# The product of p moved to the start of a decoder block, stores issued from another queue, four blocks stored as parts

## The chip, the cores and the metric

The kernel runs on one core of one Trainium2 chip. Its time is the device time of one execution in microseconds (us), and a version is judged by the median of several executions. The core has a matrix engine (TensorE, PE in the profile, with PEld for its weight loads), three engines for elementwise work (VectorE, DVE; ScalarE, ACT; GpSimd, POOL), and SyncE (SP), which here only issues DMA transfers. Each engine takes its instructions in the order of its own list and waits on semaphores; a DMA can be issued from the list of SP or, as the changed kernel does more, of POOL.

## The reference

All operands are float32. For T = 1024 tokens of width 1024 the block computes

```python
h = rms_norm(x, g_pre)
u, v, z_a, q, f, inp, z_b, a_a, a_b = split(h @ w_in)         # nine times 1024 columns
y_a = spatial_gating(gelu(u), layer_norm(gelu(v))) * silu(z_a)
y_b = rms_norm(hgrn2(silu(q), f, inp)) * silu(z_b)            # 8 heads, chunks of 32 tokens
merged = sigmoid(a_a) * (y_a @ w_branch_a) + sigmoid(a_b) * (y_b @ w_branch_b)
x = x + rms_norm(merged @ w_out, g_post)
e = p @ w_ple                                                  # (1024, 256) @ (256, 1024)
x = x + rms_norm(e * sigmoid(x @ w_ple_gate + b_ple_gate), g_ple)
```

The product e depends on the inputs p and w_ple alone and is used only in the last line.

## The kernel before

Every float32 operand of a product is split into a high part (`hi`, a cast to float32r, made by ACT at line 133) and a low part (`lo`, operand minus `hi`, made by DVE at line 134). A product is then three matmuls: high by low, low by high, high by high. The large products are made with seven block products in place of eight (`pair`): left and right sides are cut into 2 x 2 blocks, sums of blocks are formed, and the seven right-hand blocks are called b11, t4, t2, t1, t3, b21 and b22 in the order of use. Each block is a `slot`, a pair of 1 MB tiles (`...h` and `...l`), of which seven are on chip: x00, x01, x10, x11 and t0, t1, t2. One block product with a weight is 12 matmuls of 128 x 128 by 512 columns at line 748.

The stages, in order of time in the profile:

1. Start (0 to about 53 us). x is loaded in eight tiles `xt`, two per quarter, normalised by ACT and DVE, and transposed by PE (line 108) into the blocks of h. The first token product (lines 204 to 206, `token_first`) follows the transposes closely. `WARM` matmuls on zeros (line 104) stand ahead of all.
2. Token stage (to about 217 us): the columns `inp` and v of the projection, stored to DRAM as `v_sp` (line 351) and `vn_sp` (line 359) by way of token rooms `tq`. POOL forms sums of blocks of w_out and stores them (`wo_t`, line 497). DVE forms the sums of h's blocks (`sums`).
3. Projections (217 to 880 us): 28 pairs of columns in the order of the list "F0 Q0 U0 ZA0 ... ZB3 AB3", with the eight HGRN2 heads (`head`) woven in. Results go through eight buffers `q` (`quarter_tile`, QS = 8) to DRAM: f_sp, q_sp, u_sp, ga_sp, gb_sp by `stored` (line 839), bf_sp by `mix_b`, and in ZA the seven blocks of the first branch's input by `spill` (af_sp). A head reloads its F, Q and V.
4. The product e (880 to 908 us): w_ple is loaded and split into slot x00, p is loaded in pairs of token tiles into q buffers, transposed by PE, split, multiplied (lines 955 to 957), copied by ACT and stored as `e_sp`.
5. First branch (from 908 us): the seven blocks are read back by `fill`, which loads half a block into a raw buffer (three of these, RAWS = 3), and splits it into its slot; `weight_product` then runs four rounds (jp = 0 to 3) of seven block products.
6. Second branch, w_out product, gate (to 1270 us). The gate reloads e_sp.

The order of instructions on each engine comes from a scheduler that follows the order in which the program is written, with buffers and dependences as its limits. All transfers go through SP's list except the stores of `wo_t`. The splits of weights use five `hi` and five `lo` buffers (`unit`, UNITS = 5).

Of the kernel before, what the change touches and what calls it, by code (L numbers as in the profile page):

```python
# [8 lines left out]
F32 = mybir.dt.float32  # L9
# [16 lines left out]
AHEAD = 2  # L26
# [7 lines left out]
def hybrid_block(  # L34
# [45 lines left out]
    af_sp = {n: dram.tile([P, 4, 512], F32, name=f"af_{n}") for n in ("b11", "b21", "b22", "t1", "t2", "t3", "t4")}  # L80
# [153 lines left out]

    xts = [sp.tile([P, D], F32, name=f"xt{t}") for t in range(NT)]
# [103 lines left out]
    xb, xq = pool("xb", bufs=1, side="right")  # L339
# [6 lines left out]
    def to_heads(c0, g, r):  # L346

        h = c0 // P
        v = r.rearrange("p (t c) -> p t c", t=2)
        for i in range(2):  # L350
            nc.sync.dma_start(out=v_sp[h + i][:, 2 * g:2 * g + 2, :], in_=v[:, :, i * P:(i + 1) * P])

    def to_norm(c0, g, r):

        j = c0 // 256
        v = r.rearrange("p (t c) -> p t c", t=2)
        for t in range(2):
            nc.vector.bn_stats(out=stats[:, 2 * g + t, j, :], in_=v[:, t, :])
        nc.sync.dma_start(out=vn_sp[j][:, 2 * g:2 * g + 2, :], in_=v)
# [157 lines left out]
    nc.sync.dma_start(out=wT_sp, in_=wT)  # L517
# [18 lines left out]
    nc.sync.dma_start(out=badd_sp, in_=badd)  # L536
# [23 lines left out]
    def head(h):  # L560
# [170 lines left out]
        nc.sync.dma_start(out=b_sp[h], in_=z)  # L731
# [106 lines left out]
    def stored(dst, half, q):  # L838
        nc.sync.dma_start(out=dst[:, half * 512:(half + 1) * 512], in_=q)

    def projection(kind, jp):
# [21 lines left out]
        def mix_b(i, half, q):  # L863
            nc.scalar.activation(out=q, in_=q, func=AF.Silu)
            nc.vector.tensor_tensor(out=q, in0=q, in1=reload(b_sp[2 * jp + i], half), op=ALU.mult)
            nc.sync.dma_start(out=bf_sp[jp][:, i, half * 512:(half + 1) * 512], in_=q)
# [3 lines left out]
        def spill(n, t):  # L870
            nc.sync.dma_start(out=af_sp[n][:, jp, :], in_=t)
# [56 lines left out]
    wple = fill("x00", w_ple.rearrange("(k p) c -> p k c", p=P), [P, 2, D], "wple")  # L928
    first = pair_load(row_parity(w_branch_a), 0)
    pins, p_ready = {}, []  # L930

    def e_parts(t):
        if t % 2 == 0:
            pins[t // 2] = quarter_tile().rearrange("p (t c) -> p t c", t=2)
            nc.sync.dma_start(out=pins[t // 2], in_=p[t * P:(t + 2) * P, :].rearrange("(t p) c -> p t c", p=P))
        pt = small()
        for k in range(2):
            transpose(pt[:, k * P:(k + 1) * P], pins[t // 2][:, t % 2, k * P:(k + 1) * P])
        ph, pl = (a[:, 0:2, :] for a in unit(4))
        split(ph, pl, pt[:, 0:256].rearrange("p (k t) -> p k t", k=2))  # L940
        p_ready.append((ph, pl))

    for t in range(AHEAD):
        e_parts(t)
    for t in range(NT):
        if t + AHEAD < NT:
            e_parts(t + AHEAD)
        ph, pl = p_ready[t]
        pe = dense_tile()
        if t % 2 == 0:  # L950
            ev = xp.tile([P, 2, D], F32, tag=("x11h", "x11l")[t // 2 % 2], name="ev")
        for h in range(2):
            s = slice(h * 512, (h + 1) * 512)
            for k in range(2):
                nc.tensor.matmul(out=pe[h], lhsT=pl[:, k, :], rhs=wple[0][:, k, s], start=(k == 0), stop=False)
                nc.tensor.matmul(out=pe[h], lhsT=ph[:, k, :], rhs=wple[1][:, k, s], start=False, stop=False)
                nc.tensor.matmul(out=pe[h], lhsT=ph[:, k, :], rhs=wple[0][:, k, s], start=False, stop=(k == 1))
        for h in range(2):
            nc.scalar.copy(out=ev[:, t % 2, h * 512:(h + 1) * 512], in_=pe[h])
        if t % 2:  # L960
            nc.sync.dma_start(out=e_sp[t // 2], in_=ev)
# [25 lines left out]
    B = [fill(tag, bf_sp[k], [P, 2, T], f"B{k}") for k, tag in enumerate(("x01", "t1", "t0", "t2"))]  # L987
# [6 lines left out]
    for j in range(8):  # L994
# [6 lines left out]
        if j < 3:  # L1001
            n, tag = (("b11", "x10"), ("t4", "x11"), ("t2", "x00"))[j]
            o_blocks[n] = fill(tag, wo_sp[n] if j else wo[0][:, :, 0:512], [P, 4, 512], f"wo_{n}")
# [5 lines left out]
    def rest_of_blocks():  # L1009
        for n, tag, src in (("t1", "x01", wo_sp["t1"]), ("t3", "t1", wo_sp["t3"]),  # L1010
                            ("b21", "t0", wo[1][:, :, 0:512]), ("b22", "t2", wo[1][:, :, 512:1024])):
            o_blocks[n] = fill(tag, src, [P, 4, 512], f"wo_{n}")
# [23 lines left out]
    def x1T(t):  # L1036

        tag = ("t1h", "t1l", "t0h", "t0l")[t % 4]
# [9 lines left out]
    for tp in range(4):  # L1048
# [5 lines left out]
        if tp == 3:  # L1054
            wg = []
            for k, tag in enumerate(("x10", "x11", "x00", "x01")):
# [88 lines left out]
```

## Time and profile before

| | |
|---|---|
| median of 3 runs | 1273.06 us (1271.33 to 1277.49) |
| the profiled execution | 1271.88 us, its span 1270.2 us |
| PE busy | 1218.4 us, 96% of the span |
| PEld busy | 1018.5 us |
| DVE, ACT, POOL busy | 913.9, 601.4, 49.1 us |
| DMA moved | 184.07 MB, mean 145 GB/s |
| chain that ended last | PE 70%, DVE 12%, DMA 10%, ACT 5% |

The span is the time between the first and the last instruction of the profiled execution; 1.7 us of its time lie outside. A busy share is an average over all stages. The chain is the sequence of work that ended last, followed back from the end.

### The profile page before, as it was taken

Reading aid. Unit: us, or ns where it says so; the run is one execution under the profiler, and the core shown is the slowest. Engines: PE = TensorE matmul, PEld = TensorE weight load, DVE = VectorE, ACT = ScalarE, POOL = GpSimd, SP = SyncE. Lnnn points to the kernel's source line nnn. Section 1 sums busy time; section 2 is a strip of 40 time slices with the busy share of each in tenths; the row PEclk is TensorE's granted clock in tenths of the full one; section 3 lists DMA queues with packets and bytes.
Section 4 is the critical chain, followed back from the end, with each engine's and each line's share of the span. In section 5 each row is a group of like instructions: output and inputs, shape, how many; then the busy total and the mean of one; then the engine's idle time right before and its main releaser. Section 6 shows DMA issues by size and latency. Waiting matters only on the chain.

```text
span 1270.2 us, 20163 instructions
## 1 busy us (share of the span) xinstructions
PE 1218.4 (96%) x7640; PEld 1018.5 (80%) x7640; DVE 913.9 (72%) x1797; ACT 601.4 (47%) x1045; POOL 49.1 (4%) x94
## 2 busy tenths in 40 slices
PE   7899899999999999999999999999989999999997
PEld 6899898878778787887878788887768788887886
DVE  7986556678886888868686868655476753889866
ACT  5443333655665456645456545545643420545422
POOL 5025100000000000000000000000000000000000
PEclk8999989999999999999999999999989999999999
DMA  6347422435545354452443434346763771515231
GB/s 216 117 150 228 154 100 84 131 109 175 171 140 171 120 164 148 151 191 75 158 134 119 134 114 158 105 136 199 248 184 125 259 246 34 166 34 192 90 99 68
DMA packets 122966, 184.07 MB, mean 145 GB/s; under 512 B 8266, under 2 KB 76402, under 8 KB 122356
## 3 DMA queue, kind: packets, MB, share of 16 engines
q1 hardware_dynamic: 121588, 178.58, 42.8%
q0 software_dynamic: 1280, 4.20, 0.8%
q8 instruction: 60, 0.98, 0.3%
q14 instruction: 38, 0.31, 0.1%
HBM read 124.28 MB, written 58.46 MB: 144 GB/s over the span
## 4 chain that ended last, share of the span: by engine, by line
PE 70%; DVE 12%; DMA 10%; ACT 5%; issue 2%; SPq 0%; DVEq 0%; POOL 0%; ACTq 0%
PE big L748 39%; PE big L168 7%; PE small L108 2%; PE big L1078 2%; PE big L1080 2%; PE big L1079 2%; PE big L205 2%; PE big L206 2%; DVE lo L134 2%; PE big L204 2%; DMA Q<-q_sp 1%; DMA raw<-af_t 1%; PE small L205 1%; PE small L206 1%; PE small L204 1%
## 5 line engine op out<-in xcount | busy, mean ns | idle before, releaser
L134 DVE TENSOR_TENSOR lo<-S,hi 128x512 fp32r<-128x512 f32 x168 | 120.0, 718 | 83.4 <-ACT hi L133 82.2
L133 ACT CAST hi<-S 128x512 fp32r<-128x512 f32 x168 | 103.0, 618 | 153.4 <-PE big L748 100.8
L133 ACT CAST hi<-raw 128x512 fp32r<-128x512 f32 x122 | 75.1, 620 | 147.4 <-PE big L748 73.1
L134 DVE TENSOR_TENSOR lo<-raw,hi 128x512 fp32r<-128x512 f32 x122 | 83.2, 687 | 59.0 <-ACT hi L133 58.8
L771 DVE TENSOR_TENSOR q<-big,q 128x512 f32<-128x512 f32 x128 | 86.0, 685 | 12.7 <-PE big L748 11.7
L757 ACT COPY q<-big 128x512 f32<-128x512 f32 x108 | 62.8, 582 | 26.2 <-PE big L748 22.1
L752 DVE TENSOR_TENSOR S<-raw 128x512 f32<-128x512 f32 x64 | 44.0, 688 | 23.3 <-DMA raw<-in_w_in_dram 14.7
L748 PE MATMUL big<-t1l,hi 128*128 128x512 f32 x112 | 44.8, 400 | 1.9 <-ACT hi L133 1.9
L748 PE MATMUL big<-h00l,hi 128*128 128x512 f32 x112 | 45.1, 403 | 0.7 <-ACT q L757 0.7
L748 PE MATMUL big<-h11l,hi 128*128 128x512 f32 x112 | 45.3, 405 | 0.0
L748 PE MATMUL big<-t3l,hi 128*128 128x512 f32 x112 | 45.1, 403 | 0.0
L748 PE MATMUL big<-t2l,hi 128*128 128x512 f32 x112 | 45.1, 402 | 0.0
L748 PE MATMUL big<-h10l,hi 128*128 128x512 f32 x112 | 44.8, 400 | 0.0
L748 PE MATMUL big<-t0l,hi 128*128 128x512 f32 x112 | 44.8, 400 | 0.0
L748 PE MATMUL big<-t0h,hi 128*128 128x512 f32 x112 | 44.6, 398 | 0.0
L748 PE MATMUL big<-h00h,hi 128*128 128x512 f32 x112 | 44.6, 398 | 0.0
L748 PE MATMUL big<-t1h,lo 128*128 128x512 f32 x112 | 44.6, 398 | 0.0
L748 PE MATMUL big<-t0h,lo 128*128 128x512 f32 x112 | 44.5, 397 | 0.0
L748 PE MATMUL big<-t1h,hi 128*128 128x512 f32 x112 | 44.3, 396 | 0.0
L748 PE MATMUL big<-h10h,hi 128*128 128x512 f32 x112 | 44.3, 396 | 0.0
L748 PE MATMUL big<-h00h,lo 128*128 128x512 f32 x112 | 44.3, 396 | 0.0
L748 PE MATMUL big<-t2h,lo 128*128 128x512 f32 x112 | 44.1, 394 | 0.0
(559 smaller groups left out, 3691.4 us busy)
## 6 DMA issues: line engine op xcount, KB each, us to landing
raw<-in_w_in_dram SPq DMA_DIRECT2D x66, 512.0 KB, 3.9
xt<-in_x_dram SPq DMA_DIRECT2D x8, 512.0 KB, 8.9
v_sp<-tq SPq DMA_DIRECT2D x32, 128.0 KB, 3.6
wo_t<-t POOLq DMA_DIRECT2D x16, 256.0 KB, 4.0
vn_sp<-tq SPq DMA_DIRECT2D x16, 256.0 KB, 2.4
V<-v_sp SPq DMA_DIRECT2D x8, 512.0 KB, 4.5
f_sp<-q SPq DMA_DIRECT2D x16, 256.0 KB, 2.1
F<-f_sp SPq DMA_DIRECT2D x8, 512.0 KB, 3.6
```

The lines of the kernel that those rows point to most:

```text
L108: nc.tensor.transpose(out=o, in_=i, identity=ident[:n, :n])
L133: nc.scalar.copy(out=hi, in_=src)
L134: nc.vector.tensor_tensor(out=lo, in0=src, in1=hi.bitcast(F32), op=ALU.subtract)
L168: nc.tensor.matmul(out=ps[c0 // 512][:, c0 % 512:c0 % 512 + n], lhsT=wt(k), rhs=a(k, c0, n), start=(k == 0 and i == 0), stop=(k == NK - 1 ...
L204: nc.tensor.matmul(out=o, lhsT=al, rhs=hi, start=first, stop=False, **kw)
L205: nc.tensor.matmul(out=o, lhsT=ah, rhs=lo, start=False, stop=False, **kw)
L206: nc.tensor.matmul(out=o, lhsT=ah, rhs=hi, start=False, stop=last, **kw)
L748: nc.tensor.matmul(out=o, lhsT=w[:, k, :], rhs=x_[:, k, :], start=(k == 0 and i == 0 and not onto), stop=(k == 3 and i == 2), skip_group_c ...
L752: nc.vector.tensor_tensor(out=o, in0=x_, in1=y, op=op)
L757: nc.scalar.copy(out=o, in_=src)
L771: nc.vector.tensor_tensor(out=o, in0=x_, in1=y, op=ALU.add)
L1078: nc.tensor.matmul(out=o, lhsT=parts[:, 1, k, :], rhs=wh, start=(k == 0), stop=False)
```

## The change

The product e is made in the setup, quarter by quarter: `pins` (p) and the two halves of w_ple are loaded ahead of x, and a function `embedding(tp)` between the loads of a quarter of x and its normalisation makes one quarter of e and stores it. It uses buffers of the pool `xq` that the slots t1 and t2 take later. The first weights of the token stage are split with ACT's cast where DVE cast before, and the tile `sq` has one buffer where it had two. The stores v_sp, vn_sp, wT_sp, badd_sp, b_sp, bf_sp, af_sp and all of `stored` are issued by POOL (`nc.gpsimd`) where SP issued them. Four of the seven blocks of the first branch (`PARTED`) are split by `spill`, stored as two tensors, and read back by a plain DMA into their slot; the slots are handed out in another order, so that each block takes the slot that the block of the same turn had in the projections.

```diff
-AHEAD = 2
+PARTED = ("b11", "t2", "t3", "b22")
...
+    pins = xq.tile([P, NT, 256], F32, tag="t1h", name="pins")
+    wple = [sp.tile([P, 2, D], F32R, name=f"wple{n}") for n in "hl"]
+    for tp in range(4):
+        nc.sync.dma_start(out=pins[:, 2 * tp:2 * tp + 2, :],
+                          in_=p[tp * 256:(tp + 1) * 256, :].rearrange("(t p) c -> p t c", p=P))
+        if tp < 2:
+            raw = wp.tile([P, D], F32, tag="raw", name="raw", bufs=RAWS)
+            nc.sync.dma_start(out=raw, in_=w_ple[tp * P:(tp + 1) * P, :])
+            split(*(a[:, tp, :] for a in wple), raw)
+
+    def embedding(tp):
+
+        pt = small()
+        for t in range(2):
+            for k in range(2):
+                transpose(pt[:, (2 * t + k) * P:(2 * t + k + 1) * P], pins[:, 2 * tp + t, k * P:(k + 1) * P])
+        ph, pl = unit(4)
+        split(ph, pl, pt.rearrange("p (k t) -> p k t", k=4))
+        ev = xq.tile([P, 2, D], F32, tag=("t2h", "t2l")[tp % 2], name="ev")
+        for t in range(2):
+            for h in range(2):
+                pe = big()
+                s = slice(h * 512, (h + 1) * 512)
+                for k in range(2):
+                    for i, (w, a) in enumerate(((wple[0], pl), (wple[1], ph), (wple[0], ph))):
+                        nc.tensor.matmul(out=pe, lhsT=a[:, 2 * t + k, :], rhs=w[:, k, s], start=(k == 0 and i == 0),
+                                         stop=(k == 1 and i == 2))
+                nc.scalar.copy(out=ev[:, t, s], in_=pe)
+        nc.sync.dma_start(out=e_sp[tp], in_=ev)
...
+        embedding(quarter)
...
-            sq = sp.tile([P, D], F32, tag="sq", name="sq", bufs=2)
+            sq = sp.tile([P, D], F32, tag="sq", name="sq")
...
-            first.append(units_of(raw, split_dve))
+            first.append(units_of(raw, split))
...
     def stored(dst, half, q):
-        nc.sync.dma_start(out=dst[:, half * 512:(half + 1) * 512], in_=q)
+        nc.gpsimd.dma_start(out=dst[:, half * 512:(half + 1) * 512], in_=q)
...
         def spill(n, t):
-            nc.sync.dma_start(out=af_sp[n][:, jp, :], in_=t)
+            if n not in PARTED:
+                nc.gpsimd.dma_start(out=af_sp[n][:, jp, :], in_=t)
+                return
+            parts = unit(1)
+            split(*(a[:, 0, :] for a in parts), t)
+            for a, dst in zip(parts, af_parts[n]):
+                nc.gpsimd.dma_start(out=dst[:, jp, :], in_=a[:, 0, :].bitcast(F32))
...
-    for n, tag in (("b11", "x01"), ("t4", "t1"), ("t2", "t0"), ("t1", "t2"), ("t3", "x10"), ("b21", "x11"), ("b22", "x00")):
-        a_blocks[n] = fill(tag, af_sp[n], [P, 4, 512], f"a_{n}")
+    for n, tag in (("b11", "x00"), ("t4", "x01"), ("t2", "t1"), ("t1", "t0"), ("t3", "t2"), ("b21", "x10"), ("b22", "x11")):
+        if n in PARTED:
+            a_blocks[n] = slot(*at(tag), [P, 4, 512], f"a_{n}")
+            for part, src in zip(a_blocks[n], af_parts[n]):
+                nc.sync.dma_start(out=part.bitcast(F32), in_=src)
+        else:
+            a_blocks[n] = fill(tag, af_sp[n], [P, 4, 512], f"a_{n}")
```

The rest of the diff takes out the stage of the product e between the projections and the first branch, changes `nc.sync` to `nc.gpsimd` at the other stores named, and renames the slots that later blocks take.

SP's list at the start, before. Rows name what is written and what is read: `xt` are the tiles of x, `raw` buffers for weights.

```order
L96 DMA rows_g<-in_g_pre_dram 8x128
L244 DMA xt_202<-in_x_dram 128x1024
L244 DMA xt_203<-in_x_dram 128x1024
L190 DMA raw<-in_w_in_dram 128x4x256
L244 DMA xt_204<-in_x_dram 128x1024
L244 DMA xt_205<-in_x_dram 128x1024
L190 DMA raw<-in_w_in_dram 128x4x256
L244 DMA xt_206<-in_x_dram 128x1024
L244 DMA xt_207<-in_x_dram 128x1024
L244 DMA xt_208<-in_x_dram 128x1024
L244 DMA xt_209<-in_x_dram 128x1024
```

The same place in the changed kernel. `pins` is p, `ev` a finished quarter of e.

```order
L240 DMA pins<-in_p_dram 128x2x256
L244 DMA raw<-in_w_ple_dram 128x1024
L240 DMA pins<-in_p_dram 128x2x256
L244 DMA raw<-in_w_ple_dram 128x1024
L240 DMA pins<-in_p_dram 128x2x256 x2
L276 DMA xt_224<-in_x_dram 128x1024
L276 DMA xt_225<-in_x_dram 128x1024
...
L191 DMA raw<-in_w_in_dram 128x4x256
L276 DMA xt_228<-in_x_dram 128x1024
L265 DMA e_sp_142<-ev 128x2048
L276 DMA xt_229<-in_x_dram 128x1024
```

Six transfers, four of p and two of w_ple, now stand ahead of the first tile of x, and the store of the first quarter of e between x's tiles.

PE's list at the start, before: `rows_g` is g_pre, line 204 the first token product.

```order
L108 MATMUL small<-ident,rows_g 128x8
L108 MATMUL small<-ident,xt_202 128x128 x4
L108 MATMUL small<-ident,xt_203 128x128
...
L108 MATMUL small<-ident,xt_202 128x128
L108 MATMUL small<-ident,xt_203 128x128
L204 MATMUL big<-hi,h00l 128x256
L205 MATMUL big<-lo,h00h 128x256
L206 MATMUL big<-hi,h00h 128x256
```

The same place in the changed kernel; the lines left out repeat the three matmuls of line 262 or the transposes of the same two tiles.

```order
L109 MATMUL small<-ident,rows_g 128x8
L109 MATMUL small<-ident,pins 128x128 x4
L262 MATMUL big<-wpleh,lo 128x512
L262 MATMUL big<-wplel,hi 128x512
L262 MATMUL big<-wpleh,hi 128x512
...
L109 MATMUL small<-ident,xt_224 128x128 x4
L109 MATMUL small<-ident,xt_225 128x128
...
L109 MATMUL small<-ident,pins 128x128 x4
L262 MATMUL big<-wpleh,lo 128x512
...
L109 MATMUL small<-ident,xt_226 128x128
L109 MATMUL small<-ident,xt_227 128x128
```

Four transposes of p and 24 matmuls of e now stand ahead of x's first transposes, three more such lumps follow between x's quarters, and the token products (lines 205 to 207 now) come only after all of x's transposes.

SP's list between the projection AB3 and the first branch, before: `af_...` are the stored blocks of the branch's input, `gb_sp` the results of AB3.

```order
L810 DMA raw<-in_w_branch_a_dram 128x4x256 x2
L825 DMA raw<-af_b_125 128x1024 x2
L935 DMA q<-in_p_dram 128x2x256 x3
L839 DMA gb_sp_149<-q 128x512 x2
L839 DMA gb_sp_148<-q 128x512
L935 DMA q<-in_p_dram 128x2x256
L825 DMA raw<-af_t_131 128x1024
L839 DMA gb_sp_148<-q 128x512
L825 DMA raw<-af_t_131 128x1024
L961 DMA e_sp_138<-ev 128x2048
```

The same place in the changed kernel.

```order
L867 DMA q<-b_sp_75 128x512 x2
L972 DMA a_b11l<-af_b11l 128x2048
L842 DMA raw<-in_w_branch_a_dram 128x4x256
L972 DMA a_b11h<-af_b11h 128x2048
L857 DMA raw<-af_t_127 128x1024
L972 DMA a_t2h<-af_t2h 128x2048
L972 DMA a_t2l<-af_t2l 128x2048
L972 DMA a_t3h<-af_t3h 128x2048
L857 DMA raw<-af_t_127 128x1024
L857 DMA raw<-af_t_126 128x1024 x2
L972 DMA a_t3l<-af_t3l 128x2048
L857 DMA raw<-af_b_125 128x1024 x2
```

The loads of p and the stores of e and of AB3's results are gone from here, and blocks b11, t2, t3 and b22 come as two transfers each, straight into their slots (`a_b11l`, `a_b11h` and so on).

## Rows read from the trace of the kernel before

**Rows 1.** The page, part 1: busy us, share of the span, instructions.

```profile
PE 1218.4 (96%) x7640; PEld 1018.5 (80%) x7640; DVE 913.9 (72%) x1797; ACT 601.4 (47%) x1045; POOL 49.1 (4%) x94
```

**Rows 2.** Waits of PE: us in total, times, longest us.

```profile
PE small L205 <- DVE lo L134: 7.3, 2, 5.1
...
PE big L205 <- DVE lo L134: 4.4, 2, 4.1
PE big L748 <- DVE a_t1l L134: 3.3, 1, 3.3
PE big L748 <- DVE a_b21l L134: 2.3, 1, 2.3
```

**Rows 3.** Stretches: busy us (instructions) per engine, granted clock, DMA share, GB/s.

```profile
4.00:12.00 8.00, 3.95 (x7) 1.33 (x5) 4.35 (x18) 4.60 (x8) 8.00 (x30) 0.88 1.05 395
52.00:62.00 10.00, 5.93 (x38) 5.74 (x37) 10.00 (x18) 3.28 (x6) 0.00 (x0) 0.83 0.34 105
100.00:110.00 10.00, 7.82 (x55) 7.62 (x54) 9.97 (x10) 2.19 (x4) 5.93 (x7) 0.83 0.79 251
144.00:154.00 10.00, 4.89 (x29) 4.70 (x28) 5.91 (x8) 1.53 (x4) 0.00 (x0) 0.83 0.45 138
900.00:920.00 20.00, 18.32 (x82) 14.69 (x79) 9.97 (x13) 11.77 (x20) 0.00 (x0) 1.00 0.86 294
940.00:960.00 20.00, 19.86 (x87) 16.30 (x88) 15.26 (x26) 6.67 (x12) 0.00 (x0) 1.00 0.36 108
```

**Rows 4.** Timeline of PE, 880 to 939: start, us, instruction, idle before.

```profile
881.50 1.28 PE L108 MATMUL small<-ident,q 128*128 128x128 f32 x8 [1.67 <-DMA q<-in_p_dram]
883.96 0.80 PE L955 MATMUL big<-wpleh,lo 128*128 128x512 f32 x1 [1.18 <-DVE lo L134]
...
908.55 0.39 PE L748 MATMUL big<-a_b11l,hi 128*128 128x512 f32 x1
...
938.59 0.39 PE L748 MATMUL big<-a_b11l,hi 128*128 128x512 f32 x1
```

**Rows 5.** Groups of PE's instructions, 879 to 909: busy us, mean ns, idle before.

```profile
L108 PE MATMUL small<-ident,q 128*128 128x128 f32 x16 | 2.8, 276 | 1.7 <-DMA q<-in_p_dram 1.7
```

**Rows 6.** Timeline of the start, ACT and PE.

```profile
6.26 1.06 ACT L250 ACTIVATE sq<-xt 128x1024 f32<-128x1024 f32 x1 [0.21 <-DMA xt<-in_x_dram]
...
13.01 3.65 PE L108 MATMUL small<-ident,xt 128*128 128x128 f32 x16 [5.06 <-DVE xt L253]
...
56.92 0.39 PE L205 MATMUL big<-lo,h00h 128*128 128x256 f32 x1 [4.07 <-DVE lo L134]
```

**Rows 7.** The page, part 5: operands of 128 x 512, mean ns of one.

```profile
L134 DVE TENSOR_TENSOR lo<-S,hi 128x512 fp32r<-128x512 f32 x168 | 120.0, 718 | 83.4 <-ACT hi L133 82.2
L133 ACT CAST hi<-S 128x512 fp32r<-128x512 f32 x168 | 103.0, 618 | 153.4 <-PE big L748 100.8
```

**Rows 8.** DVE near 100 (timeline); waits at 138 to 156 and of SP's queue.

```profile
DVE S L399 <- DMA raw<-in_w_in_dram: 13.6, 1, 13.6
...
99.49 3.64 DVE L399 TENSOR_TENSOR S<-raw,rawx 128x1024 f32<-128x1024 f32 x1 [5.85 <-DMA raw<-in_w_in_dram]
...
SPq L359 <- ACT tq L500: 52.1, 13, 14.5
```

**Rows 9.** The page, part 6 (KB, median us to landing); POOL's groups.

```profile
wo_t<-t POOLq DMA_DIRECT2D x16, 256.0 KB, 4.0
...
f_sp<-q SPq DMA_DIRECT2D x16, 256.0 KB, 2.1
...
L497 POOL DMA_DIRECT2D wo_t<-t x16 | 9.0, 563 | 1.2 <-POOL t L172 0.9 <-DMA wo_t<-t 0.3
```

**Rows 10.** The chain at one head (start, us); DVE's waits, 217 to 880.

```profile
407.38 2.12 DMA q_sp<-q
...
409.55 4.67 DMA Q<-q_sp
...
DVE Qp L570 <- DMA Q<-q_sp: 2.4, 4, 1.5
```

More of the change, by code (lines that the diff above doesn't have):

```diff
@@ L79, in hybrid_block @@
     vn_sp = [dram.tile([P, 8, 256], F32, name=f"vn_sp{j}") for j in range(4)]
-    af_sp = {n: dram.tile([P, 4, 512], F32, name=f"af_{n}") for n in ("b11", "b21", "b22", "t1", "t2", "t3", "t4")}
+    af_sp = {n: dram.tile([P, 4, 512], F32, name=f"af_{n}") for n in ("b21", "t1", "t4")}
+    af_parts = {n: [dram.tile([P, 4, 512], F32, name=f"af_{n}{m}") for m in "hl"] for n in PARTED}
     wT_sp = dram.tile([P, 4, P], F32, name="wT_sp")
@@ L215, in slot @@
         return [pl.tile(shape, F32R, tag=f"{tag}{n}", name=f"{name}{n}") for n in "hl"]
+    xb, xq = pool("xb", bufs=1, side="right")
     blk = {(i, j): slot(xp, f"x{i}{j}", [P, 4, 512], f"h{i}{j}") for i in range(2) for j in range(2)}
@@ L350, in to_heads @@
         for i in range(2):
-            nc.sync.dma_start(out=v_sp[h + i][:, 2 * g:2 * g + 2, :], in_=v[:, :, i * P:(i + 1) * P])
+            nc.gpsimd.dma_start(out=v_sp[h + i][:, 2 * g:2 * g + 2, :], in_=v[:, :, i * P:(i + 1) * P])
     def to_norm(c0, g, r):
@@ L358, in to_norm @@
             nc.vector.bn_stats(out=stats[:, 2 * g + t, j, :], in_=v[:, t, :])
-        nc.sync.dma_start(out=vn_sp[j][:, 2 * g:2 * g + 2, :], in_=v)
+        nc.gpsimd.dma_start(out=vn_sp[j][:, 2 * g:2 * g + 2, :], in_=v)
     def values(c0, g, ps):
@@ L516, in hybrid_block @@
                             fill=0.0, base=0, channel_multiplier=-1)
-    nc.sync.dma_start(out=wT_sp, in_=wT)
+    nc.gpsimd.dma_start(out=wT_sp, in_=wT)
     lnb = kp.tile([1, D], F32, name="lnb")
@@ L535, in hybrid_block @@
         nc.vector.tensor_copy(out=badd[:, 4 * half:4 * half + 4, :].rearrange("p j t -> p (j t)"), in_=pb)
-    nc.sync.dma_start(out=badd_sp, in_=badd)
+    nc.gpsimd.dma_start(out=badd_sp, in_=badd)
     kst.close()
@@ L730, in head @@
             nc.scalar.activation(out=z[:, g * 512:(g + 1) * 512], in_=pt, func=AF.Copy, scale=qg[:, h:h + 1])
-        nc.sync.dma_start(out=b_sp[h], in_=z)
+        nc.gpsimd.dma_start(out=b_sp[h], in_=z)
         yield
@@ L865, in mix_b @@
             nc.vector.tensor_tensor(out=q, in0=q, in1=reload(b_sp[2 * jp + i], half), op=ALU.mult)
-            nc.sync.dma_start(out=bf_sp[jp][:, i, half * 512:(half + 1) * 512], in_=q)
+            nc.gpsimd.dma_start(out=bf_sp[jp][:, i, half * 512:(half + 1) * 512], in_=q)
         ya = {}
         def spill(n, t):
-            nc.sync.dma_start(out=af_sp[n][:, jp, :], in_=t)
+            if n not in PARTED:
[5 more added lines that the diff above has]
+                nc.gpsimd.dma_start(out=dst[:, jp, :], in_=a[:, 0, :].bitcast(F32))
         def mix_a(i, half, q):
@@ L926, in hybrid_block @@
     gst.close()
-    wple = fill("x00", w_ple.rearrange("(k p) c -> p k c", p=P), [P, 2, D], "wple")
     first = pair_load(row_parity(w_branch_a), 0)
[L930 to L961, printed above, removed]
-    a_blocks = {}
-    for n, tag in (("b11", "x01"), ("t4", "t1"), ("t2", "t0"), ("t1", "t2"), ("t3", "x10"), ("b21", "x11"), ("b22", "x00")):
-        a_blocks[n] = fill(tag, af_sp[n], [P, 4, 512], f"a_{n}")
+    a_blocks = {}
+    for n, tag in (("b11", "x00"), ("t4", "x01"), ("t2", "t1"), ("t1", "t0"), ("t3", "t2"), ("b21", "x10"), ("b22", "x11")):
[5 more added lines that the diff above has]
+            a_blocks[n] = fill(tag, af_sp[n], [P, 4, 512], f"a_{n}")
     mst, mp = pool("merged", bufs=1)
@@ L986, in hybrid_block @@
     first = weight_load(cols(w_branch_b, 0, 0))
-    B = [fill(tag, bf_sp[k], [P, 2, T], f"B{k}") for k, tag in enumerate(("x01", "t1", "t0", "t2"))]
+    B = [fill(tag, bf_sp[k], [P, 2, T], f"B{k}") for k, tag in enumerate(("x00", "x01", "t1", "t0"))]
     wo = row_halves(w_out)
@@ L1001, in hybrid_block @@
         if j < 3:
[L1002 removed]
+            n, tag = (("b11", "t2"), ("t4", "x10"), ("t2", "x11"))[j]
             o_blocks[n] = fill(tag, wo_sp[n] if j else wo[0][:, :, 0:512], [P, 4, 512], f"wo_{n}")
@@ L1009, in rest_of_blocks @@
     def rest_of_blocks():
-        for n, tag, src in (("t1", "x01", wo_sp["t1"]), ("t3", "t1", wo_sp["t3"]),
-                            ("b21", "t0", wo[1][:, :, 0:512]), ("b22", "t2", wo[1][:, :, 512:1024])):
+        for n, tag, src in (("t1", "x00", wo_sp["t1"]), ("t3", "x01", wo_sp["t3"]),
+                            ("b21", "t1", wo[1][:, :, 0:512]), ("b22", "t0", wo[1][:, :, 512:1024])):
             o_blocks[n] = fill(tag, src, [P, 4, 512], f"wo_{n}")
@@ L1036, in x1T @@
     def x1T(t):
-        tag = ("t1h", "t1l", "t0h", "t0l")[t % 4]
+        tag = ("x01h", "x01l", "t1h", "t1l")[t % 4]
         parts = at(tag)[0].tile([P, 2, 8, P], F32R, tag=tag, name="x1T")
@@ L1055, in hybrid_block @@
             wg = []
-            for k, tag in enumerate(("x10", "x11", "x00", "x01")):
+            for k, tag in enumerate(("t2", "x10", "x11", "x00")):
                 wg.append(fill(tag, w_ple_gate[2 * k * P:(2 * k + 2) * P, :].rearrange("(k p) c -> p k c", p=P),
```

1 line of the change is left out of this document (removed).

## The prediction

> **What bounds the kernel now.** I read the page first: TensorE (PE) is busy for 1218.4 us, 96% of the span [rows 1]. There is no other engine to relieve, so a change can win only in three ways: it takes PE work away, it fills the rest, in which PE stands, or it keeps PE out of the stretches in which its clock is granted at half. The waits of PE say where it stands [rows 2]: on the low parts of split operands at lines 205 (4.4 and 7.3 us) and, in the first branch's product, on blocks a_t1l and a_b21l (3.3 and 2.3 us). The stretches then say what each stand costs besides itself [rows 3]: where PE stood 4 to 5 us, the granted clock of the 10 us around it averages 0.83, that is, about 3.4 us at 1.2 instead of 2.4 GHz, or 1.7 us lost. The undisturbed pitch is in the stretch 940 to 960, 19.86 us for 87 matmuls of 512 columns: 0.228 us each.
>
> **The stage that goes.** PE's timeline [rows 4] shows the product of p between the last projection and the first branch. PE runs dry at 879.83 (881.50 less 1.67), stands twice (1.67 and 1.18 us), and begins the branch at 908.55. All 28.7 us go: 96 matmuls would be 21.9 us at full pitch, the rest is 16 transposes of 0.276 us [rows 5], the two stands and a slow start. That is **-28.7 us** on the path, as nothing else was waited for at 879.83.
>
> **What follows the stage.** The branch's first round, 84 matmuls, goes from 908.55 to 938.59 [rows 4]: 30.0 us for 19.2 us of work. The 10.9 us too many are the waits for blocks that are read back, split by ACT and DVE and only then used, and the half clock behind them. Afterwards, 4 of the 7 blocks come as two ready parts, and a block takes the slot of the same turn in the projection AB3 before it, so that each slot is free (12 x 0.228 =) 2.7 us after the previous one, and 16.4 us before its new block is due. The first slot is free at about 863.4, the last block is due at 863.4 + 16.4 + 16.4 = 896.2: 33 us for 3 x 1.05 + 4 x 2.10 = 11.5 MB (before: 7.3 MB). At the 395 GB/s of a saturated stretch this takes 29 us, at the 294 GB/s of the stretch 900 to 920 it takes 39 [rows 3]; a megabyte of weights for the branch goes with it. So the last blocks are between 0 and 10 us late, with half clock 0 to 14. I take 5, near the middle since both rates are seen: **-10.9 + 5 = -5.9 us** (-10.9 to +3).
>
> **Where the stage goes.** The p work now stands ahead of the token stage, in PE's order in four lumps: 4 transposes and 24 matmuls before x's first transposes, the other three between x's quarters, and the token products only behind all of them. SP issues 2.10 MB (p, w_ple) ahead of x; at 395 GB/s [rows 3] x lands 5.3 us later. Before, xt1 was there at 6.26 and PE's first x transpose at 13.01, after a stand of 5.06 us [rows 6]; afterwards that is about 18.4. The first lump fits into this longer stand: where 1.05 MB of x had landed by 6.26, the 1.57 MB up to the second half of w_ple land near 7.6, its split takes twice the 0.618 and 0.718 us of a half as long operand [rows 7], and 24 matmuls take 5.5 us, at half clock 10.9, so that it is done between 15.8 and 21.2. The other 72 matmuls cost 16.4 us, their 12 transposes 3.3: with the 5.3 this makes **+25.0 us** until the token products are done. The bounds are +20 (lumps that fill PE's waits for x's evacuation) and +34 (2.8 us of the first lump at half clock, and 6 us of waits for p's own splits: about twice the 1.18 us above in each of three lumps).
>
> **What the delay pays for.** At 52.85 to 56.92 PE waits 4.07 us for a low part [rows 6] because DVE is busy for 10.00 of 10 us [rows 3]: it makes the sums of x's blocks. DVE needs no PE result for these once x is transposed, and it now has the 22 us of the token products (192 matmuls of 256 columns at half the pitch) to do them. I take that stand and its half clock as gone: **-5.8 us** (-5.8 to 0).
>
> **The stores that move to POOL's queue.** SP's queue issues in order, so a load behind a store waits for the store's data. In the stretch 138 to 156 DVE waits 13.6 us for a weight load [rows 8], whose issue stood behind v_sp stores; SP's waits for such data reach 14.5 us. PE's stand there (5.1 us, the longest wait of line 205 [rows 2]) and its half clock are 6.8 us. With the stores away the load goes out earlier: -6.8. The stand near 102 is 2.2 us and 1.7 of clock; there DVE's sum took 3.64 us for 1024 columns, with POOL's additions beside it [rows 8], and POOL keeps them; I take half: -1.9. **Together -8.7 us** (-10.7 to 0).
>
> The Trainium skill, "SBUF - State Buffer", section "Who interferes with whom", says that a DVE instruction with two SBUF inputs contends with a GpSimd instruction that reads SBUF. By that rule the slow sum stays wherever POOL's additions fall, the -1.9 would be 0 and the sum below 1.9 us less of a gain; the 3.64 us agree with it, and no row shows additions at another place.
>
> The price: a store on POOL's queue takes 0.563 us to issue and lands after 4.0 us in the median, against 2.1 us on SP's [rows 9]. The 4.0 is from a busy stretch, so 0 to 1.9 us more apiece. Two things wait for a store. First, the reload of a head's Q, which stands in the chain of waits as 2.12 us of store and 4.67 us of load ahead of DVE [rows 10]; there are eight heads, so 0 to 15 us. Second, the eight q buffers, on which nothing waited before. DVE waits for Q in four heads alone, 2.4 us in all [rows 10]. I take **+3 us**, a little under 0.8 for each of these four (0 to 15).
>
> **Four blocks stored as parts.** Four splits per ZA projection, 16 in all, each 0.618 us of ACT and 0.718 of DVE [rows 7]: 2.9 us of DVE per ZA stage. PE does not stand in these stages, but the parts sit in the five hi and lo buffers that the weights' splits use until their stores land. **+1 us**, bounds 0 and 16 (once in each of the four stages a product that waits the 4.0 us of a store for its buffer).
>
> Sum: -28.7 - 5.9 + 25.0 - 5.8 - 8.7 + 3 + 1 = **-20.1 us**. The profiled execution took 1271.9 us, the median of the runs is 1273.1, so the sum gives 1251.8 on the first and 1253.0 on the second. Of the open terms more can go against me than for me, so I say **1254 us**.
>
> **Rivals.**
> *The start eats more.* PE takes its instructions in order, and if the lumps wait for their own splits and DVE's backlog only moves along with them, the +25.0 are +34 and the -5.8 are 0: the sum is -5.3 and the time 1268. For it: every lump begins with transposes whose split it needs at once. Against: in two of the lumps x's transposes stand between. Chance 0.14.
>
> *The reading back becomes the bound.* 11.5 MB at 294 GB/s or less, the raw buffers shared with the branch's weights: 14 us late instead of 5, so 1263. For it: raw blocks in the stage before ran at 294 GB/s. Against: DMA was asked for them late, and a part needs no raw buffer. Chance 0.10.
>
> *POOL's queue holds the buffers (slower).* If a late store makes PE stand in the 28 projections, it decides from about 0.86 us per projection (24 / 28), which cancels the 20.1 of the sum and replaces the 3 + 1 in it. Two thirds of the extra 1.9 us in each, 1.27 x 28 = 35 us, gives 1284; all of it, 1302. For it: a pair of projection products writes 8 results into 8 buffers. Against: in the projections PE stands for hardly anything now, and there is slack of a product's 2.7 us behind each buffer. Chance 0.11.
>
> The Trainium skill, same page, warning on "The DVE blocks DMA trap (SWDGE)", and "DMA: Bandwidth & Descriptors", section "SWDGE vs HWDGE vs iDMA", speak for this rival: descriptors of a POOL DMA are written by GpSimd, which is locked out while DVE runs a two-port copy. No row here shows a store held that way; if it were, the rival's times above are what it would give.
>
> *More comes back.* Lumps fill waits (+20), blocks in time (-10.9), stores free: -20.1 - 5 - 5 - 4 = -34, so 1239. Chance 0.08.
>
> **How the numbers follow.** The forecast (1246 to 1261) has 0.57. The range goes to the rivals on both sides: 1240 and 1275, leaving out most of the POOL rival and half of the last one. What a measurement here can tell from no change is about 0.5%, 6.4 us. Below 1266.7: the forecast, the last rival, most of the second: 0.74. Within 6.4 us: the first rival and the tail of the second: 0.16. Above 1279.4: the third, less its mild end: 0.10.
>
> **What will show it.** Between the last AB3 matmul and the first of the branch nothing but the pitch. The branch's first round at 20 to 25 us, with waits, if any, on the last blocks (t3, b21, b22). The first x transpose near 18, the last token product of the first kind some 25 us later than now, no 4 us stand behind it and no 5 us stand one pair later. SP's waits for ACT's q and tq gone, POOL's in their place; f_sp and q_sp landing in 2.5 to 4 us. I am wrong if PE stands inside the projections 217 to 880 for more than a few us, if the token stage is more than 20 us later at its end, or if blocks are over 10 us late.

## The result and the profile after

The changed kernel takes 1310.9 us (median of 4 runs, 1302.81 to 1312.72) against 1272.78 us before (4 runs here, 3 of them in the table of before): a ratio of 1.0281, 95% interval 1.023 to 1.0331, so it is slower by about 38 us where 1254 us was forecast. The profiled execution took 1312.72 us with a span of 1311.0 us.

The page of the changed kernel, part 1 [rows 1], and PE's waits [rows 2]:

```profile
PE 1232.4 (94%) x7640; PEld 1027.2 (78%) x7640; DVE 910.6 (69%) x1797; ACT 606.5 (46%) x1053; POOL 160.1 (12%) x292
```

```profile
PE big L780 <- ACT hi L134: 36.4, 10, 6.5
PE big L262 <- DVE lo L135: 5.7, 4, 2.8
PE small L206 <- DVE lo L135: 4.9, 1, 4.9
PE small L667 <- ACT q L789: 3.2, 3, 1.4
...
PE big L780 <- DVE a_t1l L135: 1.2, 2, 1.0
PE big L780 <- DMA a_b22l<-af_b22l: 1.2, 1, 1.2
```

PE waits 36.4 us, in ten pieces, for the cast of a weight by ACT ahead of a block product (line 748 is now 780). Before, the same wait was 1.9 us:

```profile
PE big L748 <- ACT hi L133: 1.9, 1, 1.9
```

Eight of the ten pieces, 32.7 us, stand in pairs at the ends of the four ZA projections: 2.6 us ahead of ZA's last block product, and 4.6 or 6.5 us ahead of the first product of the projection behind it. The waits on the branch's blocks a_t1l and a_b21l, 3.3 and 2.3 us before, are down to 1.2 and 0.4 us.

The table splits the span by the first matmul of a stage in PE's timeline. "Token results" is the start of ACT's fourth copy of a token product, "projections" the first matmul of F0 (209.9 us before, where the list of stages has about 217), and the length of a projection runs from its first matmul to the next one's.

| us | before | changed | difference | forecast |
|---|---|---|---|---|
| first transpose of x | 13.0 | 19.0 | +6.0 | +5.4 |
| fourth token result | 47.2 | 77.5 | +30.3 | +25.0 |
| projections begin | 209.9 | 230.9 | +21.0 | +10.5 |
| F0 to the end of AB3 | 669.8 | 719.8 | +50.0 | +4 |
| product e after AB3 | 28.8 | 0 | -28.8 | -28.7 |
| first round of the branch | 30.0 | 26.4 | -3.7 | -5.9 |
| from there to the end | 331.6 | 333.9 | +2.3 | 0 |

The last five rows of differences add up to 40.8 us, the difference of the spans. The 50 us of the projections are 60.5 in the four ZA (26.9, 23.8, 26.9 and 23.7 us before; 41.8, 38.7, 41.5 and 39.8 now), less some 10 in the projections behind them.

How such a ZA loses its time is seen in two timelines of the changed kernel at the end of ZA0, first the lines of PE that waited, then ACT:

```profile
322.91 0.50 PE L780 MATMUL big<-h11l,hi 128*128 128x512 f32 x1 [2.62 <-ACT hi L134]
323.81 0.74 PE L780 MATMUL big<-h11h,lo 128*128 128x512 f32 x1 [0.17 <-DVE lo L135]
337.71 0.79 PE L780 MATMUL big<-h00l,hi 128*128 128x512 f32 x1 [4.62 <-ACT hi L134]
```

```profile
321.72 0.62 ACT L134 CAST hi<-q 128x512 fp32r<-128x512 f32 x1 [1.05 <-DVE q L928]
322.25 0.61 ACT L134 CAST hi<-S 128x512 fp32r<-128x512 f32 x1
...
335.92 1.22 ACT L134 CAST hi<-q 128x512 fp32r<-128x512 f32 x2 [2.19 <-DVE q L176]
337.05 1.14 ACT L134 CAST hi<-raw 128x512 fp32r<-128x512 f32 x2
338.15 0.62 ACT L134 CAST hi<-S 128x512 fp32r<-128x512 f32 x1
340.10 0.62 ACT L134 CAST hi<-S 128x512 fp32r<-128x512 f32 x1 [1.33 <-DMA af_t3h<-hi]
```

`hi<-q` are casts of parts that will be stored, `hi<-raw` and `hi<-S` casts of weights. A part is cast when DVE has made its block, and the weight behind it in ACT's list has to wait. PE waits 2.62 us for the cast that begins at 322.25, and 4.62 us for the first weight of U1, which is cast at 337.05, behind two parts. The clock makes it dearer. Two stretches of the changed kernel, around ZA0's and ZA1's ends, and the one of before around ZA0's end:

```profile
320.00:342.00 22.00, 14.60 (x73) 11.84 (x72) 18.20 (x35) 10.93 (x22) 5.95 (x11) 0.84 0.66 211
376.00:406.00 30.00, 20.65 (x157) 15.34 (x156) 24.51 (x52) 17.82 (x36) 5.94 (x11) 0.83 0.47 159
```

```profile
291.00:313.00 22.00, 21.30 (x125) 17.93 (x124) 16.67 (x30) 14.31 (x29) 0.00 (x0) 1.00 0.50 153
```

A granted clock of 0.84 over 22 us is 7.0 us at 1.2 GHz, 0.83 over 30 us 10.2 us (length times twice what lacks to 1), where it was 1.00 before. What is done at half the clock takes twice as long, so half of these 17.2 us is lost, 8.6 us in two of the four ZA. At the ends of ZA2 and ZA3 (498 to 520 and 551 to 581) the clock is 0.81, by the same working 9.9 us. With the 32.7 us of waits this makes 51, close to the 50 that the projections are longer.

What ACT did before, at the same place: three weights of U1 cast far ahead of U1's first matmul.

```profile
284.39 0.62 ACT L133 CAST hi<-raw 128x512 fp32r<-128x512 f32 x1
288.03 0.62 ACT L133 CAST hi<-raw 128x512 fp32r<-128x512 f32 x1 [1.90 <-issue]
292.07 0.62 ACT L133 CAST hi<-S 128x512 fp32r<-128x512 f32 x1 [2.19 <-PE big L748]
...
302.03 0.48 PE L748 MATMUL big<-h00l,hi 128*128 128x512 f32 x1
```

The first weight of U1 was ready 17 us before PE began with it. ACT's list says the same without any time. Before, `raw_3520`, `raw_3522` and `S2_3607`, all of U1, stand ahead of the last work of ZA0 (line 879):

```order
L133 CAST hi_3528<-raw_3520 128x512
L757 COPY q_3281<-big_3179 128x512
L598 COPY sc_2645<-small_3287 32x8x32 x2
L133 CAST hi_3575<-raw_3522 128x512
L598 COPY sc_2645<-small_3326 64x8x64
L133 CAST hi_3609<-S2_3607 128x512
```

In the changed kernel U1's first weights, `raw_3731` and `raw_3733`, stand behind three parts and all of ZA0:

```order
L134 CAST hi_3672<-q_3669 128x512
L747 ACTIVATE oN_3720<-small_3723 128x512
L134 CAST hi_3700<-q_3693 128x512
L134 CAST hi_3710<-q_3706 128x512
L134 CAST hi_3739<-raw_3731 128x512
L134 CAST hi_3786<-raw_3733 128x512
```

### The profile page after: what moved, and what is told of

It is laid out like the page before. It is cut to its first block, busy times and chain, and to the rows that moved or that the text cites. A ratio compares the mean times of both kernels' runs of the same rounds, so it can differ in the third digit from the quotient of the medians.

```text
span 1311.0 us, 20290 instructions
## 1 busy us (share of the span) xinstructions
PE 1232.4 (94%) x7640; PEld 1027.2 (78%) x7640; DVE 910.6 (69%) x1797; ACT 606.5 (46%) x1053; POOL 160.1 (12%) x292
## 4 chain that ended last, share of the span: by engine, by line
PE 44%; issue 35%; POOL 6%; DMA 5%; DVE 5%; ACT 3%; SPq 0%; POOLq 0%; DVEq 0%; ACTq 0%
PE big L780 18%; PE big L169 6%; PE big L207 2%; PE big L205 2%; PE big L206 2%; PE big L1087 2%; PE big L1088 2%; PE big L1089 2%; PE big L262 1%; PE small L206 1%; PE small L207 1%; PE small L205 1%; PE small L109 1%; DVE lo L135 1%; DMA raw<-in_w_branch_a_dram 1%
## 5 line engine op out<-in xcount | busy, mean ns | idle before, releaser
L135 DVE TENSOR_TENSOR lo<-raw,hi 128x512 fp32r<-128x512 f32 x126 | 87.3, 697 | 62.9 <-ACT hi L134 62.7
L780 PE MATMUL big<-h11l,hi 128*128 128x512 f32 x112 | 47.9, 427 | 10.5 <-ACT hi L134 10.5
L780 PE MATMUL big<-h11h,lo 128*128 128x512 f32 x112 | 47.1, 421 | 0.2 <-DVE lo L135 0.2
L780 PE MATMUL big<-h11h,hi 128*128 128x512 f32 x112 | 46.4, 415 | 0.0
```

The source lines that it names most:

```text
L135: nc.vector.tensor_tensor(out=lo, in0=src, in1=hi.bitcast(F32), op=ALU.subtract)
L780: nc.tensor.matmul(out=o, lhsT=w[:, k, :], rhs=x_[:, k, :], start=(k == 0 and i == 0 and not onto), stop=(k == 3 and i == 2), skip_group_c ...
```

## The experiments

The theories. **A**: the parts cost it; they are made late in a ZA projection and stand, in ACT's list or in the five `hi` and `lo` buffers, ahead of the next weights. **B**: the stores from POOL's queue cost it; they land late and hold buffers. Ratios are to the kernel before, with 95% intervals.

**Undoing one part at a time.** First the changed kernel with no block in parts:

```diff
-PARTED = ("b11", "t2", "t3", "b22")
+PARTED = ()
```

> The changed kernel with all seven blocks of the first branch stored whole again (no block in parts); everything else as changed. Theory A (the casts and buffers of the parts delay the casts of the next weights in the four ZA projections, some 15 us each): the ZA stands go, the branch's first round goes back to about 30 us, time 1258 to 1268. Theory B (stores issued by POOL come late and hold buffers): the seven stores of a ZA and all others still go through POOL, so most of the loss stays, 1290 or more.

Measured: 1287.55 us, ratio 1.0105 (1.006 to 1.0149). ZA0 to ZA3 take 26.9, 25.5, 26.9 and 26.0 us. The first round of the branch takes 37.3 us, not 30, and the projections 682.1 us, not 669.8, so the time is above what A gave; the ZA stands are gone with POOL's stores in place, against B.

Then the parts with every moved store back on SP (nine lines of `nc.gpsimd.dma_start` to `nc.sync.dma_start`):

> The changed kernel with all moved stores issued by SP again, blocks still stored in parts. Theory A: the ZA projections still take 38 to 42 us each, time 1300 to 1315. Theory B: the stands in ZA go with the slow stores, 1255 to 1270.

Measured: 1325.15 us, ratio 1.0395 (1.0353 to 1.0438); ZA0 to ZA3 42.2, 39.5, 42.0 and 39.2 us. B falls: without POOL's stores the same projections lose the same time, and the whole is 14 us slower still.

Both undone, so that the move of e is left, with the order of the slots, ACT's casts of the first token weights and the single buffer of `sq`:

> Only the move of e to the start is left of the change (and the order of the slots): stores by SP, blocks whole. Against e1 this gives the price of POOL's queue where no parts are stored. Theory A: 1258 to 1272, near e1. Theory B: 1250 to 1262 and at least 25 us under e1. The move alone by the prediction's terms is -28.7 + 25.0 - 5.8, so about -9.5 us or 1263.

Measured: 1283.72 us, ratio 1.0083 (1.006 to 1.0107). What is left is a loss of some 11 us, not a gain of 9.5. Its projections take 669.9 us, as before, but begin at 242.1, and the first round of the branch takes 37.2 us. One stand explains a good part of the start, in PE's timeline and DVE's waits:

```profile
143.59 0.58 PE L206 MATMUL small<-lo,t3h 128*128 128x256 f32 x1 [18.20 <-DVE lo L135]
```

```profile
DVE S L431 <- DMA raw<-in_w_in_dram: 22.8, 1, 22.8
```

The weight that DVE waits for is issued by SP at 130. Ahead of it in SP's list stand two loads for POOL's additions, which wait 6.3 and 2.6 us for POOL, and v_sp stores. In the changed kernel it is issued at 125.6, between the two loads, and the same stand is 4.9 us (PE's waits above, line 206). So POOL's queue gains in the token stage: the projections begin at 230.0 in the kernel with whole blocks and POOL's stores, at 242.1 in this one.

**What in the parts costs it.** The split of a part written behind the split of the next product's weight:

```diff
         wh, wl = unit(4)
         split(wh, wl, a)
+        while later:
+            later.pop(0)()
...
+            later.append(lambda: spill_parts(n, t))
+
+        def spill_parts(n, t):
             parts = unit(1)
```

> The changed kernel with the split of a part written behind the split of the next block product's weight, so that ACT's list has the weight's cast first; same buffers, same stores by POOL. Theory A in its form 'ACT's list': the ZA stands fall to half or less, time 1265 to 1290. Theory A in its form 'the five hi and lo buffers': the parts still take every buffer in turn until their stores land, 1298 to 1315. Theory B: as the changed kernel, 1298 to 1315.

Measured: 1302.38 us, ratio 1.0222 (1.0183 to 1.0262). The ZA are back at 26.9 and 24.7 us, but U1, F1, U3 and F2 behind them take 34.8, 41.3, 35.5 and 41.8 us (27.7, 28.4, 28.1, 28.5 before): PE stands 4.79 to 6.78 us at their second block product, again for a cast of ACT. The place moved with the order and most of the loss stayed.

The casts of the parts by DVE (`split_dve` in place of `split`), so that no part is in ACT's list:

> The changed kernel with the parts' casts made by DVE in place of ACT; the same buffers, the same stores by POOL. If ACT's list is what holds PE (a part's cast waits there for DVE's result, and the cast of the next weight stands behind it), no such cast is left in ACT's list and the ZA projections with the two behind them fall from about 15 us too long to 5 or less: 1262 to 1280. If the five hi and lo buffers hold PE until the parts' stores land, they are used as before: 1295 to 1315.

Measured: 1321.27 us, ratio 1.0363 (1.031 to 1.0415); ZA0 to ZA3 39.5, 32.8, 39.4 and 31.1 us, F1 and F2 36.3 and 35.8. ACT's list as the sole cause falls. It had a share: the 2.6 us stand ahead of ZA0's last product, where the weight's cast stood behind a part's, is down to 0.9 us with the buffers as they were. The longer stands remain, in other places: 4.7 us in U1, 7.6 in F1. The short stand, and ACT's waits after the end of ZA0:

```profile
323.98 0.50 PE L780 MATMUL big<-h11l,hi 128*128 128x512 f32 x1 [0.91 <-ACT hi L134]
```

```profile
337.56 1.13 ACT L134 CAST hi<-raw 128x512 fp32r<-128x512 f32 x2
341.56 0.62 ACT L134 CAST hi<-S 128x512 fp32r<-128x512 f32 x1 [2.87 <-DVE hi L138]
343.51 0.62 ACT L134 CAST hi<-S 128x512 fp32r<-128x512 f32 x1 [1.33 <-DMA af_t3h<-hi]
```

Weights are cast only when parts have been cast (by DVE at line 138) or stored: the weights and the parts take the same buffers by turns.

The four blocks stored twice, without a split:

```diff
-            parts = unit(1)
-            split(*(a[:, 0, :] for a in parts), t)
-            for a, dst in zip(parts, af_parts[n]):
-                nc.gpsimd.dma_start(out=dst[:, jp, :], in_=a[:, 0, :].bitcast(F32))
+            for dst in af_parts[n]:
+                nc.gpsimd.dma_start(out=dst[:, jp, :], in_=t)
```

> The changed kernel with the four blocks stored twice as they are, with no split (the two parts that are read back are then the same and do not add up, which leaves out 16 splits): the transfers of the parts without their casts and without the hi and lo buffers. If casts or buffers hold PE: ZA at 27 us, 1260 to 1275. If the number of stores on POOL's queue does: ZA at 35 or more, 1290 to 1310.

Measured: 1278.08 us, ratio 1.003 (1.0006 to 1.0054); ZA0 to ZA3 26.9, 24.3, 26.9 and 25.1 us. As many bytes and stores as in the changed kernel, and no loss in ZA (F1 and F2 take 33.6 and 36.3 us). Left are the casts' own time and the buffers.

The kernel that tells these two apart keeps 16 casts by ACT, 16 subtractions by DVE and all stores on POOL, and takes the buffers away: the high part goes to a `q` buffer, the low part over the block. For this b11 and b22 are split only when the sums have read them (two calls moved, not shown).

```diff
-            parts = unit(1)
-            split(*(a[:, 0, :] for a in parts), t)
-            for a, dst in zip(parts, af_parts[n]):
-                nc.gpsimd.dma_start(out=dst[:, jp, :], in_=a[:, 0, :].bitcast(F32))
+            hi = quarter_tile()
+            split(hi.bitcast(F32R), t.bitcast(F32R), t)
+            for a, dst in zip((hi, t), af_parts[n]):
+                nc.gpsimd.dma_start(out=dst[:, jp, :], in_=a)
```

> The changed kernel with its four blocks still split by ACT and DVE and stored as parts by POOL, but without the weights' hi and lo buffers: the high part goes to one of the eight q buffers, the low part takes the place of the block itself, and b11 and b22 are split at the end of a projection, when nothing reads them any more. As many casts by ACT, as many stores. Theory ring (the parts, whose data come last in a ZA projection, stand between the weights in the order in which the five buffers are handed out, so that the next weights can't be cast ahead): ZA back to 24 to 27 us, the branch's first round at 26, so 1311 - 38 = 1265 to 1278. Theory work (the casts' own time on ACT and DVE holds PE): ZA still 35 or more, 1290 to 1315.

Measured: 1274.31 us, ratio 1.0007 (0.999 to 1.0025); ZA0 to ZA3 26.9, 23.8, 26.9 and 23.8 us, the lengths of before, and the first round of the branch 27.4 us. The loss of some 37 us is gone with the parts out of the shared buffers. PE's waits for ACT's `hi` fall to this:

```profile
PE big L780 <- ACT q L789: 9.5, 5, 2.6
...
PE big L780 <- ACT hi L134: 3.7, 2, 2.0
```

The first line is what this version still pays in U1, F1, U3 and F2: with parts in the q buffers, ACT's copy of a block product into a q buffer now stands behind the parts.

**Mixtures.** The parts cast by DVE, and only the token stage's stores on POOL:

> As the kernel before it with the parts cast by DVE, and the stores of the projections and heads by SP again; only the token stage's stores stay with POOL. If POOL's later stores cost the heads some 12 us (the difference of the projections between whole blocks stored by POOL and by SP), this is 8 to 14 us faster than that kernel: 1252 to 1270. If SP's list is again blocked by stores, it is equal or slower.

Measured: 1318.9 us, ratio 1.0364 (1.0321 to 1.0407), against 1.0363 with all stores on POOL: the expected 8 to 14 us did not come. With the parts in the weights' buffers, who issues the later stores makes no difference that shows.

On top of it x's first quarter ahead of p, and each lump of e behind its quarter's transposes:

> As the kernel before it, with the first quarter of x loaded ahead of p and w_ple and each lump of e behind the transposes of its quarter of x. The first transpose of x goes from 19 back to 13 us. If the delay of the start is PE's own work (24 to 26 us of e) plus x's later loading (6 us), the token stage ends 4 to 8 us earlier: 1246 to 1264. If PE is bound by the splits of the lumps instead, no difference.

Measured: 1321.28 us, ratio 1.0387 (1.0349 to 1.0424). PE's first transpose of x is at 12.4 us, yet the fourth token result comes at 81.8, later than with p first (77.4). In the stretch from 11 to 31 us the granted clock is 0.66, against 0.74 in the changed kernel:

```profile
11.00:31.00 20.00, 14.13 (x60) 11.57 (x60) 15.91 (x46) 14.71 (x31) 5.37 (x18) 0.66 0.69 256
```

```profile
11.00:31.00 20.00, 15.33 (x58) 11.85 (x59) 13.67 (x48) 14.90 (x31) 4.84 (x25) 0.74 0.91 323
```

The mixture that it is built on has 0.83 there. Loading x's first quarter 6 us earlier did not shorten the start; as the lumps moved with it, the two are not tried apart.

The parts in q buffers, and only the token stage's stores on POOL:

> As the kernel before it, with the stores of projections and heads by SP; only the token stage's stores stay with POOL. By the stages of the runs so far: the token stage ends at 231, the projections take 670 as with stores by SP, the first round 26 to 28, the rest 332: 1255 to 1266 us. If POOL's stores cost the heads nothing, it is equal to the kernel before it.

Measured: 1282.14 us, ratio 1.007 (1.0051 to 1.0088), 8 us slower than with all stores on POOL. Its projections take 686.1 us, 6.5 more than those with POOL's stores (679.6), F1 and F2 34.6 and 36.0 us. With this many stores SP's queue is the worse one. F1 and F2 (28.4 and 28.5 us before) take longer in all versions with parts or with POOL's stores of the projections, but for the changed kernel and the same with SP's stores, where the loss lies ahead of them, in ZA1 and ZA3. With the parts in q buffers and all stores on POOL, the 6.1 us of F1 are 3.1 in which PE stands, 1.7 lost at a granted clock of 0.95, and 1.2 of the heads' work that Q1 had before; what makes PE stand differs between the versions and was not tried apart.

The token stage's stores alone, on the kernel before (four lines):

> The kernel before with only the token stage's stores (v_sp, vn_sp, wT_sp, badd_sp) issued by POOL. By the prediction's term for these stores the stands of 5.1 and 2.2 us and their half clock go: 8.7 us, 1262 to 1267 (by half of it 1269). If POOL's additions, with stores now between them, hold back the loads of w_out and behind them the weights, nothing is gained: 1270 to 1276.

Measured: 1272.19 us, ratio 0.9996 (0.9975 to 1.0018). In the profiled execution the projections begin at 204.9 us, 5.0 earlier than in the kernel before, and the 5.1 us stand is gone from PE's waits; in the whole time no gain can be told from none. One profiled execution cannot settle it either: the part behind the first round takes 331.4 to 336.4 us in the versions here, here 335.8, before 331.6.

The parts in q buffers for t2 and t3 alone:

> As the kernel with the parts in q buffers (stores by POOL), but only t2 and t3 stored as parts; b11 and b22 whole. That kernel loses some 12 us in U1, F1, U3 and F2, where ACT's list has four casts of parts ahead of a copy that PE waits for. If the number of casts at the end of a ZA projection sets this, half of it comes back, and the first round of the branch gets 2 to 5 us longer: 1265 to 1272, the first version under the kernel before. If the q buffers held by POOL's stores set it, 1272 to 1278.

Measured: 1278.32 us, ratio 1.004 (1.0018 to 1.0062). F1 and F2 stay at 35.8 and 35.1 us and the first round goes to 30.1, so the number of casts does not set what F1 and F2 lose. No version here is shown to be faster than the kernel before; the one with four parts in q buffers equals it, and so does the kernel before with the token stage's stores on POOL.

## Why the prediction was wrong

**Four blocks stored as parts: +1 us, bounds 0 and 16.** This is the step that failed. It counted the splits' time on DVE and the wait for a store, once per stage, and took "PE does not stand in these stages" from the trace of before as if it held after. What it left out is what the five `hi` and `lo` buffers are for: before, they let ACT cast U1's first weight 17 us ahead. Handed out by turns in the order of the program, four of five go to parts whose data come last in ZA, so the weights behind can't be cast ahead. Measured: the ZA 60.5 us longer, and all projections 37.7 us longer than with whole blocks (719.8 less 682.1). That it is the buffers and not the casts' time, the stores' number or POOL is shown by four of the kernels above (SP's stores, the casts by DVE, no split, the q buffers); in the last of them b11 and b22 are also split later, which was not tried by itself. The 2.6 us stands of the four ZA, 10.5 us, come right behind the cast of b22's part, so they can be due to its place in the order; the longer stands come behind the parts of t3 and t2, which are split at the same place in both kernels. The cover was named in the text ("the five hi and lo buffers that the weights' splits use") and priced at a store's landing, not at the lead that it takes away. ACT's two lists, compared row by row, show it without any run.

**Where the stage goes: +25.0, bounds +20 and +34.** Right in mechanism, mis-sized: +30.3 at the fourth token result. x's first transpose came at 19.0 (18.4 was forecast). Of the 5.7 us that PE waits at the lumps' first matmuls (line 262 on `lo`), 2.8 lie ahead of x's first transpose, inside the stand that the forecast had there; the other 2.9 are more than it counted. This is the rival "the start eats more", which was right on this point. What the clock adds is open: from 11 to 31 it was 0.74, against 0.85 over the same stretch before, 2.2 us more lost, but the mixture with 0.83 there has its fourth token result no earlier (77.4). The consequence, that the move of e can gain only the stands around the stage (28.7 less the 25 to 30 us that PE works as before), stood in the sum, but not as plainly as it should: the move with whole blocks and SP's stores measured +11 us.

**What the delay pays for: -5.8.** Held: the stand of 4.07 us behind the first token products is gone; from the fourth token result to the fifth it is 16.3 us, where it was 21.5, so 5.2 us came back.

**The stores moved to POOL's queue: -8.7, and +3 for the price.** The gain was half there: between the fourth token result and the projections 9.3 us came back, where -5.8 and -8.7 were forecast, and 5.2 of them belong to the term above, so some 4 of the 8.7 came. PE's 2.2 us stand is gone (with SP's stores as well); the 5.1 us stand, the larger part of the -8.7, is 4.9. The prediction read the 13.6 us wait wrongly. Of the kernel before, one line of SP's waits and three of its timeline:

```profile
SPq L510 <- DMA wo_t<-t: 11.9, 3, 9.3
```

```profile
134.31 0.37 SPq L510 DMA_DIRECT2D ws<-in_gmlp_w_s_dram  x1
...
136.55 2.96 SPq L351 DMA_DIRECT2D v_sp<-tq  x4
...
141.19 0.43 SPq L190 DMA_DIRECT2D raw<-in_w_in_dram  x1
```

From 122 to 134 SP stood at the load of `ws` for POOL's stores of `wo_t`. The v_sp and vn_sp stores between `ws` and the weight that DVE waited for did not wait for data; they cost their issue, some 5 us. Moving them could win that and not the whole wait: in the kernel before with the token stage's stores on POOL, DVE's wait fell from 13.6 to 8.7 us. In the changed kernel the wait stayed, as the timeline of SP shows, where `top` and `low` are w_out's blocks for POOL's additions:

```profile
125.20 0.33 SPq L523 DMA_DIRECT2D top<-in_w_out_dram  x1
125.58 0.43 SPq L191 DMA_DIRECT2D raw<-in_w_in_dram  x1
129.71 0.33 SPq L524 DMA_DIRECT2D low<-in_w_out_dram  x1
130.08 0.44 SPq L191 DMA_DIRECT2D raw<-in_w_in_dram  x1
```

A weight that DVE waits 13.6 us for, the one issued at 125.58, stands behind a load that has to wait for POOL, whose list now holds v_sp stores between the additions. The stores of the projections land a little later than from SP's queue, f_sp after 2.4 us against 2.1 [rows 9]. Those of the parts take longer, 3.1 to 4.7 us, some above the 4.0 us that the bounds went by.

```profile
f_sp<-q POOLq DMA_DIRECT2D x16, 256.0 KB, 2.4
...
af_b22h<-hi POOLq DMA_DIRECT2D x4, 256.0 KB, 4.7
```

So the rival "POOL's queue holds the buffers" ended on the right side for a wrong reason: with the stores on SP the kernel is slower still. The Trainium skill, "SBUF - State Buffer", warning on "The DVE blocks DMA trap (SWDGE)", has the descriptors of a POOL store starve while DVE runs a two-port copy. The 0.3 us between 2.4 and 2.1 show nothing of that here, but these runs hardly try it: in the projections copies take some 2 us of DVE's time, and most of the rest is TENSOR_TENSOR.

With whole blocks and POOL's stores the projections take 682.1 us against 669.9 with SP's, 12 us more, most of it in ZA1, F1, U3, ZA3 and F2; the bound of 0 to 15 held, the +3 was low.

**The stage that goes and what follows.** -28.7 was -28.8, and the first round went from 30.0 to 26.4 us, where 24.1 was forecast; it moved 379 GB/s with the DMA share at 1.01, which points to the rival "the reading back becomes the bound". That whole blocks take 37.3 us shows a term that was not in the text: before, the stage of e covered the first loads of the branch. The first of its blocks was asked for 39.4 us ahead of the branch's first matmul, in the kernel with whole blocks and POOL's stores 14.4 us ahead. The order of the slots changed with it and was not tried apart.

```profile
950.00:977.00 27.00, 21.52 (x88) 15.76 (x86) 15.52 (x20) 10.60 (x15) 1.67 (x4) 1.00 1.01 379
```

## What to carry to other kernels

A ring of buffers that lets one engine work ahead is a resource of its own: before something else may draw from it, ask when the new user's data come and who is next in turn, and price the lead that is lost, not only the time that the buffer is held. Moving work that the bounding engine must do anyway gains at most the stands around its old place, here 28.7 us less 21.9 of matmuls and 2.8 of transposes [rows 5], so 4, and it loses what the old place covered. Moving stores from one queue to another wins what they themselves held up there: look up on what the queue's waits end before pricing it, and what the new queue's other work feeds.

## What the hardware showed

The clock raised the price of short waits: around ZA0's end of the changed kernel PE stood 2.62 and 4.62 us, and of the 22 us in question it was granted 1.2 GHz for 7.0, another 3.5 us lost. And 256 KB stores of POOL's queue, in stages in which DVE is busy most of the time, landed not far from those of SP's queue: in the kernel with whole blocks 2.5 us for f_sp, 4.4 for af_b and 2.7 for af_t, against 2.1, 3.5 and 3.2 before.
